# Router logits of a mixture of experts: activations stationary in fp32, or split weights stationary with two tiles' rows streaming

## The chip, the core and the metric

The kernel runs on one core of a Trainium2 chip. The metric is the device time of one launch in microseconds (us). Three launches of the kernel before took 1594.85, 1598.17 and 1599.75 us, and their median, 1598.17 us, is the time before. Engines are named as in the profile: PE is TensorE, PEld its weight loads, DVE VectorE, ACT ScalarE, POOL GpSimd, and SP SyncE, which here only issues DMAs.

## What is computed

One decoder layer on 1024 rows of 2048 columns: a modulated norm, an input projection, spatial gating and stick-breaking attention, an output projection with a residual, and a mixture of 32 experts of which each row takes two. The part around the change is the output projection and the router:

```python
x = x + gate1 * (y @ w_out[l])                                  # y: (1024, 1024), w_out: (1024, 2048)
h = rms_norm(x, norm2_g[l]) * (1.0 + scale2) + shift2
...
g_logits = hf @ w_group + b_group                               # 4 groups
g_idx = argmax(g_logits)
e_logits = (hf @ w_route + b_route).reshape(n, 4, 8)            # 32 experts
top_val, top_idx = top_k(e_logits[g_idx], 2)
...
x = x + gate2 * m                                               # m: the two experts' outputs, weighted
```

All of it is float32. A large product is made in three passes of a split type (float32r): each factor becomes a high part (a copy that is rounded) and a low part (the rest), and high x high, high x low and low x high are summed.

## The kernel before, in words

The output projection is a plan of 32 tiles, `plan = [(cg, t) ...]`: four column groups cg of 512 columns, and in each the eight row tiles t of 128 rows. Below, tile i stands for (cg, t) with i = 8 cg + t. For each tile `mm_out` issues 24 matmuls of 512 columns, three passes for each of eight row chunks of `w_out` (n_ = 0 to 7), and between these eight steps it calls what the dictionary `between` holds. Then `evac_out` and `Piece` take the tile out on VectorE: og = acc x gate1, xi = x + og (the new residual), u = xi x arow (the row for the router and the experts, before its norm). `prev.store` sends xi and u to memory.

The order of all this is written out by hand and recorded under a manual schedule; every engine takes its instructions in that order. In column groups 0 to 2 the piece of the tile before is turned behind step 3 (`turn`: four transposes on PE and a copy uT on ACT) and its logits are made behind step 5 (`logits`: four chunks of 128 columns, the turned rows stationary, 36 columns of router weights streaming, in float32, which PE runs as two passes each). In column group 3 these stand behind steps 2 and 4, and the routing of the tiles before stands among them (`Tail`: `pick1` and `pick2` on VectorE, `exps`, `ranks`, `weights`, `onehots`). All logits are summed in one PSUM bank `lg`, 36 columns for each row tile.

Beside this the same stage also does the following. VectorE makes the experts' output gate (`Gate2.step`, four accumulations of 128x512 at each of the tiles 3 to 18; `Gate2.turn` at tiles 7, 11, 15 and 19, and at tile 19 the last sums go back through PE). `wo_split` prepares the next column group's weights (a high part on ACT, a low part on VectorE): one piece behind tiles 1 and 3 of a group, and two in the middle of tile 7 (`split_late`). `wo_gate` scales the last group's weights on VectorE in column group 2. In column group 0 `ya_turn` brings in the gMLP's rows, with a subtraction on GpSimd for each tile. At tile 8 VectorE makes the router's bias sums cbs, and TensorE uses them ahead of tile 9.

SyncE's queue holds the loads and stores of column groups 0 to 2 and behind them the experts' weights `wx`, 1 MB at a time, in twelve buffers that take the memory of the projection's pools as these come free. GpSimd's queue holds the loads and stores of group 3 and the gathers of the experts' rows. Experts then run one after the other: gather, scale, transposes, three-pass gate and up products, and the down product.

The lines that the following speaks of: `mm_out` L867; og and xi L881 to L884, u L895; the turn L906 and its copy L908; logits L913; the gate's steps L951 and their transposes L936; wo_split's copy L835 and low part L836; gMLP low part L854; cbs L1120 and its product L1124; pick1's first step L990; weights' loads L1240 and L1247; the gather L1220.

Of the kernel before, what the change touches and what calls it, by code (L numbers as in the profile page):

```python
# [17 lines left out]
P = 128  # L18
# [40 lines left out]
def body(ctx, tc, A, out):  # L59
# [580 lines left out]
    with ExitStack() as c3:  # L640
# [4 lines left out]
        class Chain:  # L645
# [78 lines left out]
            def fin0(self):  # L724
                self.y = op.tile([P, 512], F32, name="u3", bufs=3)
                SC.activation(self.y, self.yp, AF.Copy)
                self.sq = op.tile([P, 512], F32, name="og")
                SC.activation(self.sq, self.y, AF.Square)
# [91 lines left out]

    ws_ = c2.enter_context(tc.tile_pool(name="ws", bufs=6, reuse_waits="tile"))
    c5 = ExitStack()
    rt = c5.enter_context(tc.tile_pool(name="rt", bufs=1, side="right", reuse_waits="tile"))
# [66 lines left out]
    class Piece:  # L890
        def __init__(self, cg, t, x, g):
            self.cg, self.t, self.g = cg, t, g
            cs = slice(cg * 512, (cg + 1) * 512)
            self.u = op.tile([P, 512], F32, name="u3", bufs=3)
            V.tensor_tensor(self.u, x, arow[:, cs], op=ALU.mult)  # L895
            self.x = x
# [6 lines left out]
        def turn(self):  # L903
            p = pot.tile([P, 4, P], F32, name="tr2")
            for j in range(4):
                T.transpose(p[:, j, :], self.u[:, j * P:(j + 1) * P], ident)  # L906
            self.uT = self.g.rearrange("p (j q) -> p j q", j=4)
            SC.activation(self.uT, p, AF.Copy)  # L908

        def logits(self):  # L910
            for j in range(4):
                c = self.cg * 4 + j
                T.matmul(lg[:, self.t * 36:(self.t + 1) * 36], self.uT[:, j, :], wgr[:, c, :],  # L913
                         start=(self.t == 0 and c == 0), stop=(c == 15), skip_group_check=True)


    class Gate2:
        def __init__(self):
            self.n, self.t, self.p = 0, [], None
            self.acc = big.tile([P, 8, HALF], F32, name="xk")  # L920
            for i in range(2):
                self.load(i)
# [15 lines left out]
        def step(self):  # L938
# [14 lines left out]
            elif self.n == 16:  # L953
                p = pot.tile([P, 4, P], F32, name="tr2")
                T.transpose(p[0:16, 0, :], g2c, ident)
                r = self.acc[0:16, 1, 0:P]
                SC.activation(r, p[0:16, 0, :], AF.Copy)
                SY.dma_start(mod_d[M_G2:M_G2 + 1, :].rearrange("o (c p) -> (o c) p", p=P), r)
            self.n += 1

    class Tail:
# [24 lines left out]
        def pick1(self):  # L986
            t = self.t
            self.el = rt.tile([P, 36], F32, name="el", bufs=3)
            el = self.el
            V.scalar_tensor_tensor(el, lg[:, t * 36:(t + 1) * 36], self.r, cB, op0=ALU.mult, op1=ALU.add)  # L990
            yield
# [80 lines left out]
    if True:  # L1072
# [19 lines left out]
        wo_load(5)  # L1092
        lg = pol.tile([P, 512], F32, name="lg")

# [11 lines left out]
        for i in range(2):  # L1106
            xin[plan[i]] = x_in(*plan[i])
        tails, prev = {}, None
        g2 = Gate2()
        for i, (cg, t) in enumerate(plan):  # L1110
            if i + 2 < len(plan):
# [26 lines left out]
            x = xin.pop((cg, t))  # L1138
            between = {3: prev.turn, 5: prev.logits} if prev else {}
            if i >= 3 and g2.n <= 16:  # L1140
# [3 lines left out]
            if cg < 3 and t == 7:  # L1144
# [7 lines left out]
                between[4] = split_late(None, cg * 4 + 6)  # L1152
                between[5] = split_late(between[5], cg * 4 + 7)
            if cg == 3:
                between = {2: prev.turn, 4: prev.logits}
                if t >= 2:
                    between[3] = tails[t - 2].exps
# [7 lines left out]
            for n in (4, 5, 6) if i == 0 else ():  # L1165
                fin(n)
            prev = Piece(cg, t, x, evac_out(cg, t, acc, x))
            if cg < 3:
# [358 lines left out]
```

## Time and profile before

| | |
|---|---|
| median of three launches | 1598.17 us (1594.85 to 1599.75) |
| the profiled execution's own time | 1600.44 us |
| its span, first to last instruction | 1598.6 us |
| mean granted clock of TensorE | 0.977 |
| PE busy | 1510.7 us, 95% of the span |
| DVE busy | 1214.8 us, 76% |
| ACT busy | 956.8 us, 60% |
| POOL busy | 299.3 us, 19% |
| logits, L913 | 256 matmuls, 32.2 us busy, 681.7 to 914.8 us |

All times in the rows below are from this one profiled execution, in us from the span's start, and single operations in ns or us as the row says. A granted clock of 1.00 is 2.4 GHz, 0.50 is 1.2 GHz. In a timeline a row is: start, duration, engine, line, operation, output<-inputs, shape, count, and in brackets the idle time of the engine before it with what ended it. The rows of a timeline merge equal neighbours, so the distance between two starts says more of TensorE's pace than a duration, since its matmuls overlap. The output projection lies between 661 and 911 us, the experts between 931 and 1590 us.

### The profile page before, as it was taken

What the parts mean: (1) busy time and instruction counts of PE and PEld (TensorE: products, weight loads), DVE (VectorE), ACT (ScalarE), POOL (GpSimd) and SP (SyncE); (2) the same over time, 40 slices, a digit from 0 to 9 for tenths busy, and PEclk for the clock granted to TensorE, in tenths of its full rate; (3) what the DMA queues carried; (4) which work ended last, traced back from release to release, by engine and by line L of the source; (5) the groups of instructions that cost most, each with busy time, mean ns of one, the idle gap of its engine ahead of it and who ended that gap; (6) DMA issues with size and microseconds to landing.
All of it is one profiled execution on the core that took longest, in us unless ns stands there. A gap on an engine that the chain in (4) does not pass through costs nothing.

```text
span 1598.6 us, 21113 instructions
## 1 busy us (share of the span) xinstructions
PE 1510.7 (95%) x6706; PEld 1137.5 (71%) x6706; DVE 1214.8 (76%) x2214; ACT 956.8 (60%) x2032; POOL 299.3 (19%) x277
## 2 busy tenths in 40 slices
PE   5999998999999899899999879999999999999996
PEld 4788887788888655488878766666666666666663
DVE  5889675867787598758765778888888888887783
ACT  5442588764544598522223477777777777776671
POOL 2000132010011234220001213232211122313021
PEclk9899999999999999999999979999999999999998
DMA  9987478678876000468857559999999999999992
GB/s 378 353 323 239 156 253 300 237 245 295 299 267 228 31 1 1 159 210 297 293 187 290 211 217 329 366 364 377 356 382 355 363 361 355 351 373 346 353 320 37
DMA packets 94408, 433.92 MB, mean 271 GB/s; under 512 B 13088, under 2 KB 13200, under 8 KB 64208
## 3 DMA queue, kind: packets, MB, share of 16 engines
q1 hardware_dynamic: 82000, 377.54, 64.0%
q0 software_dynamic: 12000, 52.85, 11.3%
q10 hardware_dynamic: 288, 2.10, 0.3%
q8 instruction: 55, 0.90, 0.2%
q14 instruction: 65, 0.53, 0.1%
HBM read 400.16 MB, written 43.02 MB: 277 GB/s over the span
## 4 chain that ended last, share of the span: by engine, by line
PE 69%; DMA 10%; ACT 7%; issue 6%; DVE 5%; POOL 2%; SPq 0%; POOLq 0%; ACTq 0%; DVEq 0%; another core or an unknown queue 0%
PE acc L323 22%; PE gu L1291 16%; PE dn L1314 10%; PE acc L867 10%; DMA out<-y,idx 4%; DMA xg<-u_d,idx 3%; PE tp L1265 3%; DMA wm<-in_w_mod 2%; PE lg L913 1%; DVE macc L183 1%; PE tr L906 1%; PE z L657 1%; POOL sl L685 1%; ACT junk L348 1%; ACT wh L1281 1%
## 5 line engine op out<-in xcount | busy, mean ns | idle before, releaser
L1282 DVE TENSOR_TENSOR wl<-wx,wh 128x1024 fp32r<-128x1024 f32 x256 | 309.5, 1219 | 14.6 <-ACT wh L1281 13.5
L1281 ACT ACTIVATE wh<-wx 128x1024 fp32r<-128x1024 f32 x256 | 273.5, 1071 | 37.5 <-PE gu L1291 35.9
L1314 PE MATMUL dn<-wx,actT 128*128 128x512 f32 x512 | 241.5, 595 | 3.1 <-DMA wx<-in_w_down 2.5
L1291 PE MATMUL gu<-wh,xh 128*128 128x512 f32 x512 | 239.4, 468 | 0.0
L183 DVE SCALAR_TENSOR_TENSOR macc<-wm,sc_c,macc 128x512 f32<-128x512 f32 x296 | 222.1, 750 | 11.1 <-DMA wm<-in_w_mod 2.9
L323 PE MATMUL acc<-wh,hh 128*128 128x512 f32 x640 | 209.7, 398 | 3.3 <-ACT hh L279 1.8
L323 PE MATMUL acc<-wl,hh 128*128 128x512 f32 x640 | 206.8, 393 | 2.8 <-DVE wl L308 2.6
L323 PE MATMUL acc<-wh,hl 128*128 128x512 f32 x640 | 206.1, 392 | 0.8 <-DVE hl L280 0.8
L1291 PE MATMUL gu<-wl,xh 128*128 128x512 f32 x512 | 203.1, 397 | 0.2
L1291 PE MATMUL gu<-wh,xl 128*128 128x512 f32 x512 | 202.1, 395 | 0.0
L1224 POOL DMA_INDIRECT out<-y,idx x52 | 94.2, 1812 | 446.6 <-DVE y L1315 440.5
L867 PE MATMUL acc<-wo,yh 128*128 128x512 f32 x512 | 171.3, 416 | 0.0
L1315 DVE TENSOR_TENSOR y<-dn,gate 128x512 f32<-128x512 f32 x128 | 88.5, 691 | 107.8 <-PE dn L1314 107.8
L1270 ACT ACTIVATE xh<-tp,b2c 128x128 fp32r<-128x128 f32 x512 | 146.5, 383 | 21.5 <-PE tp L1265 21.5
L1314 PEld LDWEIGHTS dn<-wx,actT 128*128 128x128 f32 x512 | 96.5, 189 | 79.2 <-issue 63.0
L1272 DVE SCALAR_TENSOR_TENSOR xl<-tp,b2c,xh 128x128 fp32r<-128x128 f32 x512 | 143.3, 343 | 4.3 <-ACT xh L1270 4.3
L323 PEld LDWEIGHTS acc<-wl,hh 128*128 128x128 f32 x640 | 120.9, 190 | 30.0 <-DVE wl L308 4.9
L323 PEld LDWEIGHTS acc<-wh,hl 128*128 128x128 f32 x640 | 121.2, 189 | 27.3 <-DVE hl L280 1.5
L323 PEld LDWEIGHTS acc<-wh,hh 128*128 128x128 f32 x640 | 119.1, 189 | 27.3 <-ACT hh L279 1.9
L308 DVE TENSOR_TENSOR wl<-w,wh 128x1024 fp32r<-128x1024 f32 x80 | 97.5, 1220 | 33.9 <-ACT wh L307 33.8
L307 ACT ACTIVATE wh<-w 128x1024 fp32r<-128x1024 f32 x80 | 82.9, 1053 | 63.7 <-PE acc L323 51.8
L1291 PEld LDWEIGHTS gu<-wl,xh 128*128 128x128 f32 x512 | 97.4, 190 | 30.5 <-issue 14.8
(248 smaller groups left out, 2290.3 us busy)
## 6 DMA issues: line engine op xcount, KB each, us to landing
wx<-in_w_gu SPq DMA_DIRECT2D x128, 1024.0 KB, 23.6
wm<-in_w_mod SPq DMA_DIRECT2D x160, 512.0 KB, 5.5
wx<-in_w_down SPq DMA_DIRECT2D x64, 1024.0 KB, 22.0
w<-in_w_in SPq DMA_DIRECT2D x80, 512.0 KB, 5.4
x<-in_w_mod SPq DMA_DIRECT2D x16, 1024.0 KB, 6.7
wo<-in_w_out SPq DMA_DIRECT2D x16, 512.0 KB, 4.9
xi<-in_x SPq DMA_DIRECT2D x24, 256.0 KB, 6.2
out<-xi SPq DMA_DIRECT2D x24, 256.0 KB, 4.8
```

What stands on the lines that cost most here:

```text
L183: V.scalar_tensor_tensor(self.acc, t[:, j, :], sc, self.acc, op0=ALU.mult, op1=ALU.add)
L308: V.tensor_tensor(wl, w, wh.bitcast(F32), op=ALU.subtract)
L323: T.matmul(accs[t], a, b, start=(first and j == 0 and n == 0), stop=(last and j == 1 and n == 2))
L867: T.matmul(acc, y[a][:, c, ts_], w[b][:, c % 2, :], start=(n_ == 0 and i == 0), stop=(n_ == 7 and i == 2))
L1224: return G.indirect_dma_start(out=out, out_offset=bass.IndirectOffsetOnAxis(ap=idx, axis=0), in_=y, in_offset=None, bounds_check=S - 1, oo ...
L1270: SC.activation(xh[:, j, :], self.p[:, j, :], AF.Identity, bias=b2c[:, b * 4 + j:b * 4 + j + 1])
L1272: V.scalar_tensor_tensor(xl[:, j, :], self.p[:, j, :], b2c[:, b * 4 + j:b * 4 + j + 1], xh[:, j, :].bitcast(F32), op0=ALU.add, op1=ALU.sub ...
L1281: SC.activation(self.wh[q], w, AF.Copy)
L1282: low = lambda: V.tensor_tensor(self.wl[q], w, self.wh[q].bitcast(F32), op=ALU.subtract)
L1291: T.matmul(self.gu, a[c // 4][:, c % 4, :], b[q][:, k, :], start=(c == 0 and i == 0), stop=(c == 15 and i == 2))
L1314: T.matmul(d, self.aT[:, f, :], self.wd[f][:, cs], start=(f == 0), stop=(f == 1))
L1315: V.tensor_tensor(self.y[:, cs], d, gate2[:, cs], op=ALU.mult)
```

## The change

For the first three column groups the logits are made the other way round. The router's weights are split once into a high and a low part, side by side (`whl`: 36 + 36 columns for each of twelve chunks), and are the stationary factor. `turn` now also copies the turned rows in the split type (h, on ACT) and subtracts (l, on GpSimd), into a buffer `pair` with room for two row tiles. Behind step 1 of every odd tile `logits2` streams both tiles' rows, 256 columns: for each of four chunks one matmul of h with all 72 columns and one of l with the 36 high ones. The sums stand turned, 72 partitions by 512 rows, in two banks `lgT`. At tile 25 the last pair is made (`last`), ACT copies both banks to SBUF, and `fold` turns them back by eight float32 matmuls with two stacked identities (`two`), which also adds the high and the low part; column group 3 adds its logits on top as before. At tile 25 these logits stand behind step 6, at tile 24 there are none.

Buffers: the gate's sums move to a new small pool `lp`, and `pair` and `whl` take the memory in which they stood (`g2.parts`); u3 has two buffers in place of three; the attention's last rows y use the ring xi.

```diff
             def fin0(self):
-                self.y = op.tile([P, 512], F32, name="u3", bufs=3)
+                self.y = op.tile([P, 512], F32, name="xi", bufs=4)
...
+    lp = c2.enter_context(tc.tile_pool(name="lp", bufs=1, reuse_waits="tile"))
...
-            self.u = op.tile([P, 512], F32, name="u3", bufs=3)
+            self.u = op.tile([P, 512], F32, name="u3")
...
             self.uT = self.g.rearrange("p (j q) -> p j q", j=4)
+            if self.cg < 3:
+                h, l = (a[:, :, self.t % 2 * P:self.t % 2 * P + P] for a in pair)
+                SC.activation(h, p, AF.Copy)
+                SC.activation(self.uT, p, AF.Copy)
+                G.tensor_tensor(l, self.uT, h.bitcast(F32), op=ALU.subtract)
+                return
             SC.activation(self.uT, p, AF.Copy)
+        def logits2(self):
+            o = lgT[self.t // 4][:, (self.t % 4 - 1) * P:(self.t % 4 + 1) * P]
+            for j in range(4):
+                c = self.cg * 4 + j
+                T.matmul(o[0:72], whl[:, c, :], pair[0][:, j, :], start=(self.t % 4 == 1 and c == 0),
+                         stop=False, skip_group_check=True)
+                T.matmul(o[0:36], whl[:, c, 0:36], pair[1][:, j, :], start=False, stop=(c == 11),
+                         skip_group_check=True)
...
-            self.acc = big.tile([P, 8, HALF], F32, name="xk")
+            self.parts = big.tile([P, 8, HALF], F32R, name="xk")
+            self.acc = lp.tile([P, 1, 512], F32, name="gacc")
...
+        SC.activation(whl[:, :, 0:36], wgr[:, 0:12, :], AF.Copy)
+        G.tensor_tensor(whl[:, :, 36:72], wgr[:, 0:12, :], whl[:, :, 0:36].bitcast(F32), op=ALU.subtract)
+        G.tensor_tensor(two, ident[:, 0:36], ident[:, 36:72], op=ALU.add)
...
-            between = {3: prev.turn, 5: prev.logits} if prev else {}
+            between = {3: prev.turn} if prev else {}
+            if i == 2:
+                lgT[0] = py.tile([P, 512], F32, name="yp")
+            if i >= 3 and i % 2:
+                between[1] = older.logits2
...
                 between[4] = split_late(None, cg * 4 + 6)
-                between[5] = split_late(between[5], cg * 4 + 7)
+                between[5] = split_late(None, cg * 4 + 7)
             if cg == 3:
                 between = {2: prev.turn, 4: prev.logits}
+                if t == 0:
+                    between = {2: prev.turn}
+                if t == 1:
+                    def fold():
+                        lgq.append(pol.tile([P, 512], F32, name="lg"))
+                        for k in range(NT):
+                            T.matmul(lgq[0][:, k * 36:(k + 1) * 36], lgs[0:72, k * P:(k + 1) * P], two[0:72, :],
+                                     start=(k == 0), stop=False, skip_group_check=True)
+
+                    def last():
+                        older.logits2()
+                        for h in range(2):
+                            SC.activation(lgs[0:72, h * HALF:(h + 1) * HALF], lgT[h][0:72, :], AF.Copy)
+                    lgs = gate1[:, 0:S]
+                    between = {0: last, 2: prev.turn, 4: fold, 6: prev.logits}
...
-            prev = Piece(cg, t, x, evac_out(cg, t, acc, x))
+            older, prev = prev, Piece(cg, t, x, evac_out(cg, t, acc, x))
```

The order on three engines, first TensorE at the beginning of tile 9 (the tiles acc; cbs is the bias product ahead of it, tr the turn of tile 8, lg the logits). Before:

```order
L1124 MATMUL acc_6524<-cbs,cst 128x36 x2
L867 MATMUL acc_6528<-wo,yh_4731 128x512 x2
...
L906 MATMUL tr_6541<-cst,u_6512 128x128 x4
L867 MATMUL acc_6528<-wo,yh_4731 128x512 x2
L867 MATMUL acc_6528<-wo,yl_4732 128x512
L867 MATMUL acc_6528<-wo,yh_4731 128x512 x2
L867 MATMUL acc_6528<-wo,yl_4732 128x512
L913 MATMUL lg<-wgr,og 128x36 x4
```

And now, where xk holds whl and the pair of tiles 6 and 7, and the bank lg the turned sums:

```order
L1150 MATMUL acc_6541<-cbs,cst 128x36 x2
...
L868 MATMUL acc_6545<-wo,yh_4731 128x512 x2
L868 MATMUL acc_6545<-wo,yl_4732 128x512
L923 MATMUL lg<-xk 72x256
L925 MATMUL lg<-xk 36x256
L923 MATMUL lg<-xk 72x256
L925 MATMUL lg<-xk 36x256
...
L868 MATMUL acc_6545<-wo,yh_4731 128x512 x2
...
L907 MATMUL tr_6566<-cst,u_6529 128x128 x4
```

Four float32 products behind step 5 are gone (they stood in each tile), and eight products of 256 columns stand behind step 1 of each odd tile, ahead of the turn.

ScalarE from tile 6's evacuation to tile 8's (og<-tr is the copy uT, wo the two late weight splits, og,xss the row sums at an evacuation). Before:

```order
L885 ACTIVATE og,xss_5907<-xi 128x512
L908 ACTIVATE og<-tr_6411 128x512
L835 ACTIVATE wo<-wo 128x1024 x2
L885 ACTIVATE og,xss_5908<-xi 128x512
L908 ACTIVATE og<-tr_6486 128x512
```

And now, with the new copy h written to xk:

```order
L886 ACTIVATE og,xss_5910<-xi 128x512
L911 ACTIVATE xk<-tr_6432 128x4x128
L912 ACTIVATE og<-tr_6432 128x512
L836 ACTIVATE wo<-wo 128x1024 x2
L886 ACTIVATE og,xss_5911<-xi 128x512
```

One copy more stands between the turn and the two weight splits.

SyncE's first loads of expert weights, with the engines whose semaphores each waits for (DMAHW are its own earlier transfers). Before:

```order
L1240 DMA wx<-in_w_gu 128x2048 [waits DMAHW6_49,PE_49]
L1240 DMA wx<-in_w_gu 128x2048 [waits DMAHW7_49]
L1240 DMA wx<-in_w_gu 128x2048 [waits DMAHW0_49]
L1240 DMA wx<-in_w_gu 128x2048 [waits DMAHW1_49]
L1240 DMA wx<-in_w_gu 128x2048 [waits DMAHW2_49,PE_49]
L1240 DMA wx<-in_w_gu 128x2048 [waits DMAHW3_49]
...
L1240 DMA wx<-in_w_gu 128x2048 [waits DMAHW4_49,Activation_49]
L1240 DMA wx<-in_w_gu 128x2048 [waits DMAHW5_49,PE_49]
L1247 DMA wx<-in_w_down 128x2048 [waits DMAHW6_49,PE_49]
```

And now:

```order
L1285 DMA wx<-in_w_gu 128x2048 [waits DMAHW6_49,PE_49,Pool_49]
L1285 DMA wx<-in_w_gu 128x2048 [waits DMAHW7_49]
L1285 DMA wx<-in_w_gu 128x2048 [waits DMAHW0_49]
L1285 DMA wx<-in_w_gu 128x2048 [waits DMAHW1_49]
L1285 DMA wx<-in_w_gu 128x2048 [waits DMAHW2_49]
L1285 DMA wx<-in_w_gu 128x2048 [waits DMAHW3_49,PE_49]
...
L1285 DMA wx<-in_w_gu 128x2048 [waits DMAHW4_49]
L1285 DMA wx<-in_w_gu 128x2048 [waits DMAHW5_49]
L1292 DMA wx<-in_w_down 128x2048 [waits DMAHW6_49]
```

The first load now waits for the last pair product and GpSimd's subtraction before it. The sixth waits for TensorE's matmul of the last tile for which the twelfth waited before; the sixth to the twelfth wait for nothing else.

## Rows read from the trace of the kernel before

**Rows 1.** The page, busy time by engine (share, instructions).

```profile
PE 1510.7 (95%) x6706; PEld 1137.5 (71%) x6706; DVE 1214.8 (76%) x2214; ACT 956.8 (60%) x2032; POOL 299.3 (19%) x277
```

**Rows 2.** Stretches: PE, PEld, DVE, ACT, POOL busy; clock, DMA share, GB/s.

```profile
780.00:810.00 30.00, 30.00 (x162) 25.26 (x161) 25.57 (x35) 8.14 (x15) 0.00 (x0) 1.00 0.86 288
...
1000.00:1060.00 60.00, 60.00 (x247) 41.48 (x246) 49.76 (x87) 45.34 (x91) 15.07 (x10) 1.00 1.01 369
```

**Rows 3.** Timeline of PE around one tile's logits.

```profile
765.97 0.98 PE L913 MATMUL lg<-wgr,og 128*128 128x36 f32 x8
766.77 0.71 PE L867 MATMUL acc<-wo,yh 128*128 128x512 f32 x2
767.32 0.40 PE L867 MATMUL acc<-wo,yl 128*128 128x512 f32 x1
767.55 0.63 PE L867 MATMUL acc<-wo,yh 128*128 128x512 f32 x2
768.02 0.39 PE L867 MATMUL acc<-wo,yl 128*128 128x512 f32 x1
```

**Rows 4.** Timeline of PE in the attention, split type, 256 columns.

```profile
546.79 0.28 PE L710 MATMUL cum<-sh,comp_r 128*128 128x256 f32 x1
546.91 0.28 PE L711 MATMUL cum<-sl,comp_r 128*128 128x256 f32 x1
```

**Rows 5.** Timelines of POOL and DVE, with and without a GpSimd subtraction.

```profile
720.48 1.84 POOL L854 TENSOR_TENSOR yl<-yld,yh 128x512 fp32r<-128x512 f32 x1 [4.98 <-ACT yh L853]
...
719.65 4.01 DVE L951 SCALAR_TENSOR_TENSOR xk<-x,sc_c,xk 128x512 f32<-128x512 f32 x4
...
726.62 3.11 DVE L951 SCALAR_TENSOR_TENSOR xk<-x,sc_c,xk 128x512 f32<-128x512 f32 x4
```

**Rows 6.** Timeline of DVE, column group 0, then group 2.

```profile
712.84 3.99 DVE L951 SCALAR_TENSOR_TENSOR xk<-x,sc_c,xk 128x512 f32<-128x512 f32 x4
716.99 0.69 DVE L881 TENSOR_TENSOR og<-acc,xk 128x512 f32<-128x512 f32 x1 [0.16 <-PE acc L867]
...
803.63 0.69 DVE L881 TENSOR_TENSOR og<-acc,xk 128x512 f32<-128x512 f32 x1 [0.72 <-PE acc L867]
...
810.48 0.69 DVE L881 TENSOR_TENSOR og<-acc,xk 128x512 f32<-128x512 f32 x1 [0.55 <-PE acc L867]
```

**Rows 7.** Timelines of DVE and PE, tiles 7 to 9.

```profile
729.65 2.35 DVE L836 TENSOR_TENSOR wo<-wo 128x1024 fp32r<-128x1024 f32 x2
...
733.37 0.69 DVE L895 TENSOR_TENSOR u<-xi,xk 128x512 f32<-128x512 f32 x1
...
734.45 0.60 PE L906 MATMUL tr<-cst,u 128*128 128x128 f32 x4
...
739.78 0.41 PE L1124 MATMUL acc<-cbs,cst 128*128 128x36 f32 x2 [0.63 <-DVE cbs L1120]
```

**Rows 8.** Timeline of PE, waits behind tiles 19 and in 24.

```profile
820.55 0.27 PE L955 MATMUL tr<-cst,g2c 128*16 128x128 f32 x1 [2.75 <-DVE g2c L942]
...
852.60 0.63 PE L906 MATMUL tr<-cst,u 128*128 128x128 f32 x4 [0.45 <-DVE u L895]
```

**Rows 9.** Timeline of DVE, choice of group and evacuation at tile 25.

```profile
862.50 0.25 DVE L990 SCALAR_TENSOR_TENSOR el<-lg,rs_col,cB 128x36 f32<-128x36 f32 x1 [2.99 <-PE lg L913]
...
865.73 0.69 DVE L895 TENSOR_TENSOR u<-xi,xk 128x512 f32<-128x512 f32 x1
```

**Rows 10.** Timeline of SyncE's queue, the experts' first weights.

```profile
852.89 27.11 SPq L1240 DMA_DIRECT2D wx<-in_w_gu  x8
880.10 0.86 SPq L1247 DMA_DIRECT2D wx<-in_w_down  x2
...
911.12 0.33 SPq L1240 DMA_DIRECT2D wx<-in_w_gu  x1
```

**Rows 11.** The chain that ended last; then DMA issues, 1360 to 1420, us to landing.

```profile
924.89 5.47 DMA xg<-u_d,xss
...
xg<-u_d,idx POOLq DMA_INDIRECT x6, 12.0
```

More of the change, by code (lines that the diff above doesn't have):

```diff
@@ L912, in logits @@
                 c = self.cg * 4 + j
-                T.matmul(lg[:, self.t * 36:(self.t + 1) * 36], self.uT[:, j, :], wgr[:, c, :],
-                         start=(self.t == 0 and c == 0), stop=(c == 15), skip_group_check=True)
+                T.matmul(lgq[0][:, self.t * 36:(self.t + 1) * 36], self.uT[:, j, :], wgr[:, c, :],
+                         start=False, stop=(c == 15), skip_group_check=True)
     class Gate2:
@@ L955, in step @@
                 T.transpose(p[0:16, 0, :], g2c, ident)
-                r = self.acc[0:16, 1, 0:P]
+                r = self.acc[0:16, 0, 0:P]
                 SC.activation(r, p[0:16, 0, :], AF.Copy)
@@ L989, in pick1 @@
             el = self.el
-            V.scalar_tensor_tensor(el, lg[:, t * 36:(t + 1) * 36], self.r, cB, op0=ALU.mult, op1=ALU.add)
+            V.scalar_tensor_tensor(el, lgq[0][:, t * 36:(t + 1) * 36], self.r, cB, op0=ALU.mult, op1=ALU.add)
             yield
@@ L1092, in body @@
         wo_load(5)
-        lg = pol.tile([P, 512], F32, name="lg")
+        lgT = [None, pol.tile([P, 512], F32, name="lg")]
         def lockstep(gens):
@@ L1107, in body @@
             xin[plan[i]] = x_in(*plan[i])
-        tails, prev = {}, None
+        tails, prev, older, lgq = {}, None, None, []
         g2 = Gate2()
+        pair = [g2.parts[:, k:k + 2, :].rearrange("p a (b q) -> p (a b) q", b=2) for k in (0, 2)]
+        whl = g2.parts[:, 4:6, :].rearrange("p a n -> p (a n)")[:, 0:12 * 72].rearrange("p (c e) -> p c e", c=12)
+        two = lp.tile([P, 36], F32, name="two")
+        SC.activation(whl[:, :, 0:36], wgr[:, 0:12, :], AF.Copy)
+        G.tensor_tensor(whl[:, :, 36:72], wgr[:, 0:12, :], whl[:, :, 0:36].bitcast(F32), op=ALU.subtract)
+        G.tensor_tensor(two, ident[:, 0:36], ident[:, 36:72], op=ALU.add)
         for i, (cg, t) in enumerate(plan):
```

## The prediction

> **What bounds the kernel now.** I read the table of stretches first, then the timeline of each engine in the output projection, then the queue of SyncE. In the projection TensorE is busy 30.00 of 30 us, VectorE 25.57, and the DMA engines 0.86 [rows 2]; among the experts TensorE is busy 60.00 of 60 us with the DMA engines at 1.01 [rows 2]. So TensorE sets the end in both, its 1510.7 us [rows 1] have hardly a gap, and what the projection gains or loses goes straight to the end, as long as the experts' first rows arrive as they do now. VectorE is the engine to watch: in column group 0 it idles 0.16 us before a tile's evacuation, in group 2 0.55 us, with tiles 6.85 us apart [rows 6].
>
> **What goes from TensorE.** One tile's logits are 8 passes: from 765.97 to 766.77, 0.80 us, and the pair of matmuls behind them takes 0.55 instead of 0.47 (767.55 to 768.02), so 0.88 us [rows 3]. 24 pieces lose them: 24 x 0.88 = 21.1 us.
>
> **What comes to TensorE.** Twelve pair products of 8 matmuls, 256 columns each, in the split type. The trace has such matmuls in the attention: they start 0.12 us apart [rows 4], with 128 stationary columns, where the new ones have 72 or 36. So 0.96 us and again 0.09 for the change of stream: 1.05 us. Bounds: 0.85 us if the narrower stationary is cheaper, 1.9 us if each took the 0.235 us of half a 512-column pair [rows 3]; I take the row of the same width. 12 x 1.05 = 12.6 us. The turning back is 8 matmuls of two passes each with 36 columns, as the old logits: 16 x 0.10 + 0.08 = 1.7 us (1.2 if they cost less behind each other). Sum on TensorE: -21.1 + 12.6 + 1.7 = **-6.8 us**. Even tiles become 0.88 shorter, odd tiles 0.17 longer.
>
> **What comes to the others.** ScalarE makes one more 512-column copy per piece, some 0.5 us. It has room, but its order matters at three tiles, below. GpSimd gets 24 subtractions of 128x512; the same operation takes 1.84 us in the trace, next to VectorE [rows 5]. The buffer changes (u3 two deep, the attention's rows in xi, the small pool lp) move no wait that I find: the rows that they delay are asked for a tile later, and an x tile lands long before. They cost nothing while that holds, and a few tenths if not.
>
> **The price of the subtractions.** Four accumulation steps of the gate vector take 3.11 us on VectorE when GpSimd is idle (726.62), and 4.01 us when GpSimd's subtraction at 720.48 falls among them [rows 5]; 3.99 us at 712.84 [rows 6]. So one subtraction among such steps costs VectorE 0.90 us. This is the Trainium skill's rule in "SBUF — State Buffer", section "Who interferes with whom": a VectorE instruction with both inputs in SBUF contends with a GpSimd instruction that reads SBUF. The rows above agree. By its opposite, that only VectorE's copies meet GpSimd, these subtractions would cost nothing and the sum would end at the first rival. Nearly each of the new subtractions of tiles 3 to 19 falls among the steps: the transposes stand 2.8 us into a tile (3.85 in an odd one, behind the pair product), two copies and the semaphores later it is 4.7 (5.7), and VectorE's steps and weight low parts run from about 2.2 to 5.3 us and on to 6.5 us where a low part follows.
>
> **Where it reaches the path.** VectorE needs 2.1 us for evacuation (three operations of 0.69 [rows 6, 7]), 3.1 for the steps, up to 1.2 for a low part or a weight scaling, and now 0.9: up to 7.3 us against a mean tile of 6.5 on TensorE. Place by place:
> - Tiles 3 to 6, group 0. VectorE also scales the gMLP rows here and has 0.16 us left [rows 6]. Three subtractions add 2.7 us. By the plain sum tile 8 would start 3.0 us earlier (7 x 0.88 - 3 x 1.05); with VectorE as the pace I expect it 0.5 later. Loss 3.5.
> - Tiles 7 to 9. Tile 7's turn stands 1.05 later behind the pair product and ScalarE has the extra copy 0.5, so its two weight splits come 1.55 later and VectorE's low parts (729.65) 1.25 later; then u, now ready at 734.06, is ready at 735.4, where TensorE wants it at 734.6 (734.45 now) [rows 7]. TensorE already waits 0.63 us at 739.78 for VectorE's sums cbs [rows 7], and one more subtraction falls before them: VectorE is 2.3 later where TensorE would be 0.7 earlier. Loss 3.0 for both.
> - Tile 16, the same splits without cbs: loss 1.2.
> - Tiles 17 to 19: VectorE idles 0.55 us [rows 6], and each tile adds 0.9 where TensorE takes 0.4 less in the mean; the wait of 2.75 us at 820.55 for the gate's last sums [rows 8] hangs on the same engine. Loss 3.0.
> - Tile 24, the same splits: the wait of 0.45 us at 852.60 [rows 8] grows by 1.4.
> - Tile 26: tile 24's logits move behind the turning back, from the fifth place of tile 25 to the seventh. VectorE's choice of the group starts behind the logits, at 862.50, and runs until the evacuation, 2.5 us; that evacuation's u stands at 865.73 [rows 9]. In the changed order it starts 0.5 us before the tile's end. Loss 1.4.
> Sum of the losses 13.5 us, bounds 0 and 16: none if VectorE keeps up everywhere, 16 if every subtraction costs its 0.9. I take 13.5, since the rows with such a collision are of these very instructions. Projection: -6.8 + 13.5 = **+6.7 us**.
>
> **The experts' weights.** Of the first twelve loads eight go out from 852.89, two at 880.10, one behind them, and the twelfth at 911.12, with the projection's last matmul [rows 10]. In the changed program the order of the buffers is another: five loads are free early in column group 3, the sixth waits for the matmul for which the twelfth waits now, and seven queue behind it on SyncE. These are 7.3 MB; at the 369 GB/s of rows 2 they take 20 us from the last matmul. The weights themselves should be in time, as expert 0's four are among the five early ones and expert 1 comes an expert later. But the gather of expert 0's rows is issued 13.8 us after it and stands on the path with 5.47 us; among full queues gathers land after 12.0 us in the median [rows 11]. So the gather costs between 0 and 6.5 us more; I take **+2.5**, since only the last third of the burst meets it. The Trainium skill ("DMA: Bandwidth & Descriptors", section "Queues, rings and completion order") says that each DMA engine goes round-robin between its queues by packets; by that the gather would share and not queue behind all seven, which bears the middle value out. No row here shows the arbitration itself.
>
> **Sum.** +6.7 + 2.5 = +9.2 us on the profiled execution's 1600.44 us, so 1609.6. That execution is 2.3 us above the median of 1598.17, so against the median I say **1607 us**.
>
> **Rivals.**
> 1. GpSimd's subtractions don't hold VectorE up, or fall beside the steps. Then only the late splits (0.8 at tile 8, 1.2 at cbs, 0.8 at tile 16, 1.4 at tile 24) and tile 26 (1.4) remain, 5.6 us: -6.8 + 5.6 + 2.5 = +1.3, that is 1599.5. For it: VectorE has 4.4 us of 30 free in rows 2. Against: rows 5.
> 2. Faster: TensorE keeps its gain. VectorE catches up within a tile, since three evacuation buffers let TensorE run ahead and the turn stands well into a tile; the gather is not held up either. -6.8, so 1591.4. It decides if VectorE's idle time before an evacuation in group 2 stays above 0. For it: TensorE is busy without a gap in rows 2 although VectorE is nearly full there. Against: the turn needs the last u, so TensorE may run ahead by 2.8 us at most.
> 3. The burst is worse than I think: the gather takes the 12.0 us of full queues, +6.5 in place of +2.5, and the projection stands as forecast: 1611. For it: seven loads on SyncE's queue at once. Against: the burst has at most 6 us left when the gather starts.
>
> **Chances.** Forecast 0.45, rival 1 0.28, rival 2 0.14, rival 3 0.13. A measurement here can tell about 0.3%, 4.8 us, from no change. Rival 2 is faster by that; rival 1 lies within; forecast and rival 3 are slower, but the forecast's lower edge, where a third of its losses is missing, falls within: faster 0.14, same 0.32, slower 0.54. Forecast's own range 1602 to 1612. For 8 in 10 I take 1594 to 1613: below lies most of rival 2, above only a gather and all collisions together.
>
> **What would show it.** Pair products 0.12 us apart; VectorE's four steps near 4.0 us in most tiles of groups 0 to 2; its idle time before og gone in tiles 4 to 7 and 17 to 19; TensorE waiting for u at tiles 8, 16, 24 and 26 and longer for cbs; five weight loads before the projection's end, seven behind it; the gather longer than 5.5 us. I am wrong if the steps stay at 3.1 us, if the pair products start 0.2 us apart, or if TensorE waits for the subtractions themselves, which end about 1 us before they are wanted.

## The result, and the profile after

The changed kernel takes 1606.64 us (median of 7 runs, 1603.3 to 1610.91), the kernel before 1596.74 us (7 runs, 1593.23 to 1599.75): a ratio of 1.0068, 95% interval 1.0051 to 1.0084, so 8 to 13 us slower. The profiled execution of the changed kernel took 1606.64 us, its span is 1604.9 us. Line numbers below are those of the changed kernel: L923 and L925 the pair products, L913 GpSimd's subtraction, L970 the gate's steps, L882 and L885 the first operation of an evacuation (og, and xi in group 3), L896 u, L907 the turn, L1192 the fold.

Busy time by engine, after (share of the span, instructions), to be read against [rows 1]:

```profile
PE 1499.7 (93%) x6626; PEld 1124.1 (70%) x6626; DVE 1228.2 (77%) x2214; ACT 969.4 (60%) x2059; POOL 334.5 (21%) x303
```

TensorE is busy 11.0 us less on this page (by the distances of its rows the saving is 8.2 us, below) and the kernel is slower, so the gain turned into waits. The longest waits of TensorE from 660 to 925 us, after (engine, line <- waited for: us in total, times, longest):

```profile
PE tr L907 <- ACT og L886: 6.1, 6, 2.1
PE tr L974 <- DVE g2c L961: 3.4, 1, 3.4
PE tr L907 <- DVE u L896: 3.1, 3, 1.6
...
PE acc L1150 <- DVE cbs L1146: 2.8, 2, 2.2
```

The first line is a trap in reading. The turn doesn't need ScalarE's row sum og; it needs u, which VectorE ends at about the same moment. Where the profile names u, the turn follows its end by 0.06 us (below: u from 872.46 to 873.15, turn at 873.21, while that tile's row sum ends only at 873.24) or by 0.15 us (726.42 and 726.57); where it names og, the turn stands 0.15 us behind the end of u as well (855.96 and 856.11). So the first and the third line are one wait, for VectorE's evacuation. Before the change all waits for u came to 2.0 us in two places.

The pair products, the fold and two late turns in TensorE's timeline, after (start, duration, engine, line, operation, output<-inputs, in brackets the idle time before):

```profile
856.11 0.63 PE L907 MATMUL tr<-cst,u 128*128 128x128 f32 x4 [2.07 <-ACT og L886]
...
860.81 0.28 PE L923 MATMUL lg<-xk 128*72 128x256 f32 x1
860.92 0.28 PE L925 MATMUL lg<-xk 128*36 128x256 f32 x1
...
861.74 0.62 PE L868 MATMUL acc<-wo,yh 128*128 128x512 f32 x2
...
864.97 1.87 PE L1192 MATMUL lg<-two,xk 72*128 72x36 f32 x16
866.68 0.70 PE L868 MATMUL acc<-wo,yh 128*128 128x512 f32 x2
...
869.50 0.40 PE L868 MATMUL acc<-wo,yl 128*128 128x512 f32 x1
...
873.21 0.66 PE L907 MATMUL tr<-cst,u 128*128 128x128 f32 x4 [1.21 <-DVE u L896]
```

Pair products start 0.11 to 0.12 us apart, one of the 96 waits for GpSimd, for 0.2 us, and the next tile product comes 0.93 us after the first of the eight (861.74); the fold takes 1.71 us until 866.68. The row of 869.50 is the last product of tile 25. Tile 24's wait, 0.45 us in [rows 8], is 2.07 us, and tile 26 has a new one of 1.21 us. VectorE at that place, after, to be read against [rows 9]:

```profile
869.23 0.26 DVE L1009 SCALAR_TENSOR_TENSOR el<-lg,rs_col,cB 128x36 f32<-128x36 f32 x1 [7.04 <-PE lg L931]
...
871.74 0.68 DVE L885 TENSOR_TENSOR xi<-xi,acc 128x512 f32<-128x512 f32 x1
872.46 0.69 DVE L896 TENSOR_TENSOR u<-xi,xk 128x512 f32<-128x512 f32 x1
```

VectorE is idle for 7.04 us, then the choice of the group fills the last 2.5 us before the evacuation, which starts 1.8 us after the end of TensorE's last product of the tile (869.50 + 0.40). Now VectorE and GpSimd in group 0, after, against [rows 5, 6]:

```profile
719.44 4.93 DVE L970 SCALAR_TENSOR_TENSOR gacc<-x,sc_c,gacc 128x512 f32<-128x512 f32 x4
724.29 0.68 DVE L882 TENSOR_TENSOR og<-acc,xk 128x512 f32<-128x512 f32 x1
725.73 0.69 DVE L896 TENSOR_TENSOR u<-xi,xk 128x512 f32<-128x512 f32 x1
726.34 4.03 DVE L970 SCALAR_TENSOR_TENSOR gacc<-x,sc_c,gacc 128x512 f32<-128x512 f32 x4
```

```profile
720.27 1.86 POOL L855 TENSOR_TENSOR yl<-yld,yh 128x512 fp32r<-128x512 f32 x1 [3.95 <-ACT yh L854]
722.08 1.74 POOL L913 TENSOR_TENSOR xk<-og,xk 128x512 fp32r<-128x512 f32 x1
728.46 1.37 POOL L913 TENSOR_TENSOR xk<-og,xk 128x512 fp32r<-128x512 f32 x1 [4.63 <-ACT og L912]
```

Two GpSimd subtractions inside four steps make them 4.93 us, one makes them 4.03, none 3.11 [rows 5]: 0.90 to 0.92 us each. Taken one by one, the second and third of the four steps of 719.44 show where it falls:

```profile
720.22 0.75 DVE L970 SCALAR_TENSOR_TENSOR gacc<-x,sc_c,gacc 128x512 f32<-128x512 f32 x1
721.01 1.67 DVE L970 SCALAR_TENSOR_TENSOR gacc<-x,sc_c,gacc 128x512 f32<-128x512 f32 x1
```

The step that is running when a subtraction starts (720.27) keeps its 0.75 us; the next one, which starts while the subtraction runs, takes 1.67. So a subtraction lengthens one step. The bracket before og is gone: VectorE goes from steps to evacuation to steps without a pause.

The chain at the gather, and SyncE's weight loads, after, against [rows 10, 11]:

```profile
931.57 9.53 DMA xg<-u_d,xss
```

```profile
861.97 2.41 SPq L1285 DMA_DIRECT2D wx<-in_w_gu  x5
...
917.76 0.80 SPq L1285 DMA_DIRECT2D wx<-in_w_gu  x2
918.13 0.91 SPq L1285 DMA_DIRECT2D wx<-in_w_gu  x2
919.08 1.20 SPq L1292 DMA_DIRECT2D wx<-in_w_down  x2
920.32 29.13 SPq L1285 DMA_DIRECT2D wx<-in_w_gu  x4
```

Five loads go out early. Seven stand behind the last matmul: three by the rows of 917.76 and 918.13 (they share a load, since they come from neighbouring stretches), two of 919.08, and the first two of the last row. The gather takes 9.53 us in place of 5.47. It starts 6.68 us later than before, by the projection, and ends 10.74 us later.

The end of the span is only 6.3 us later. From the gather's end to the end of the span the changed kernel takes 663.8 us, the kernel before 668.2. The difference is a wait for a down-projection weight, in the profile of before near 1485 us, which the profile after lacks:

```profile
1485.14 1.12 PE L1314 MATMUL dn<-wx,actT 128*128 128x512 f32 x2 [2.50 <-DMA wx<-in_w_down]
```

It is taken up with the last experiment. The medians, 9.9 us apart, agree with projection and gather, 10.7 us.

### The profile page after: what moved, and what is told of

Same layout as the page of the kernel before. It is cut to its first block, busy times and chain, and to the rows that moved or that the text cites. A ratio compares the mean times of both kernels' runs of the same rounds, so it can differ in the third digit from the quotient of the medians.

```text
span 1604.9 us, 21036 instructions
## 1 busy us (share of the span) xinstructions
PE 1499.7 (93%) x6626; PEld 1124.1 (70%) x6626; DVE 1228.2 (77%) x2214; ACT 969.4 (60%) x2059; POOL 334.5 (21%) x303
## 4 chain that ended last, share of the span: by engine, by line
PE 63%; DMA 11%; DVE 9%; ACT 8%; issue 6%; POOL 2%; SPq 0%; POOLq 0%; DVEq 0%; ACTq 0%; another core or an unknown queue 0%
PE acc L323 22%; PE gu L1336 16%; PE dn L1359 10%; PE acc L868 6%; DMA out<-y,idx 4%; DMA xg<-u_d,idx 3%; PE tp L1310 3%; DMA wm<-in_w_mod 2%; DVE gacc L970 2%; DVE macc L183 1%; PE z L657 1%; ACT junk L348 1%; POOL sl L685 1%; DMA u_d<-u 1%; ACT xh L1315 1%
## 5 line engine op out<-in xcount | busy, mean ns | idle before, releaser
L1327 DVE TENSOR_TENSOR wl<-wx,wh 128x1024 fp32r<-128x1024 f32 x256 | 309.7, 1220 | 15.9 <-ACT wh L1326 14.7
L1298 ACT ACTIVATE xg<-xg,rs 128x512 f32<-128x512 f32 x126 | 92.3, 734 | 44.4 <-DMA xg<-u_d,idx 36.1
```

The costliest lines, as they stand in the source:

```text
L1298: SC.activation(xs, xs, AF.Copy, scale=self.rs)
L1327: low = lambda: V.tensor_tensor(self.wl[q], w, self.wh[q].bitcast(F32), op=ALU.subtract)
```

## Experiments

Each was timed against the kernel before in the same session; ratios have their 95% interval, and line numbers in a run's rows are those of its own kernel. The changed kernel was timed in an earlier session, so a difference from it, or between two edited kernels of different sessions, is one between sessions (medians of the kernel before: 1596.14 to 1597.35 us). Where it is below about 5 us, the rows beside it carry more than the medians. "Tile 9 at 750.53" is the start of that tile's evacuation.

**The subtraction alone, taken away.**

```diff
                 SC.activation(self.uT, p, AF.Copy)
-                G.tensor_tensor(l, self.uT, h.bitcast(F32), op=ALU.subtract)
...
+        for k in (2, 3):
+            G.tensor_tensor(g2.parts[:, k, :], gate1[:, 0:HALF], gate1[:, 0:HALF], op=ALU.subtract)
```

> The changed kernel without the 24 GpSimd subtractions (the low part of the turned rows is written once, as zero, so the logits lack it); ScalarE's two copies stay. Theory (each subtraction that falls among VectorE's two-SBUF steps costs VectorE 0.9 us, and VectorE paces the projection): the four-step groups go back to 3.1 us, the projection ends 7 to 9 us earlier than in the changed kernel, 1598 to 1600 us. Rival (the turn that stands behind the pair product and ScalarE's extra copy make the delay, not the subtraction): steps shorten, but the time stays within 2 us of 1606.6.

Measured: 1598.68 us, ratio 1.0019 (1.0006 to 1.0031), 8.0 us less than the changed kernel. The steps, in this kernel:

```profile
716.69 4.02 DVE L969 SCALAR_TENSOR_TENSOR gacc<-x,sc_c,gacc 128x512 f32<-128x512 f32 x4
722.68 3.11 DVE L969 SCALAR_TENSOR_TENSOR gacc<-x,sc_c,gacc 128x512 f32<-128x512 f32 x4
```

The first still has the gMLP rows' own subtraction among it; the other is back at 3.11 us. From tile 0 to tile 7 this kernel takes 53.10 us, the changed one 57.21. TensorE does the same work in both, so the 8.0 us are what the 24 subtractions cost. The gather still takes 9.85 us here. The rival is out.

**The subtraction alone, added to the kernel before.**

```diff
             SC.activation(self.uT, p, AF.Copy)
+            if self.cg < 3:
+                G.tensor_tensor(g2.acc[:, 2, :], self.g, arow[:, 0:512], op=ALU.subtract)
```

> The kernel before with one GpSimd subtraction of 128x512 added in each of the 24 turns of groups 0 to 2, into a tile that nobody reads. Theory: steps of 4.0 us, VectorE late by 0.9 per tile where it has 0.16 us (group 0, tiles 3 to 6) and 0.55 us (tiles 17 to 19) to spare: about 3 + 1 to 2 + 1 = 4 to 6 us slower, 1600.7 to 1602.7 us. Rival (VectorE catches up within a tile, three evacuation buffers): within 1 us of 1596.7.

Measured: 1600.67 us against 1596.67, ratio 1.0039 (1.0024 to 1.0053), the lower edge of what was expected. Its profiled execution, 1595.36 us, is the shortest of its runs; in it too the projection is longer, 240.37 us from tile 0 to tile 31 against 236.04. Two step groups of VectorE and the GpSimd work near them:

```profile
723.31 4.01 DVE L953 SCALAR_TENSOR_TENSOR xk<-x,sc_c,xk 128x512 f32<-128x512 f32 x4
...
740.13 3.11 DVE L953 SCALAR_TENSOR_TENSOR xk<-x,sc_c,xk 128x512 f32<-128x512 f32 x4
```

```profile
725.00 1.76 POOL L910 TENSOR_TENSOR xk<-og,xk 128x512 f32<-128x512 f32 x1 [4.21 <-ACT og L908]
...
742.78 1.59 POOL L910 TENSOR_TENSOR xk<-og,xk 128x512 f32<-128x512 f32 x1 [8.03 <-ACT og L908]
```

The subtraction at 725.00 lies inside the steps and they take 4.01 us; that at 742.78 starts while the last of them is already running, and they take 3.11. A result that nobody reads costs the kernel 4.0 us.

**The low part on VectorE.**

```diff
                 SC.activation(h, p, AF.Copy)
-                SC.activation(self.uT, p, AF.Copy)
-                G.tensor_tensor(l, self.uT, h.bitcast(F32), op=ALU.subtract)
+                V.tensor_tensor(l, p, h.bitcast(F32), op=ALU.subtract)
```

> The changed kernel with the low part taken by VectorE, straight from PSUM (turned rows minus high part), and neither GpSimd's subtraction nor ScalarE's second copy. Theory (what counts is VectorE's time): 24 x 0.69 = 16.6 us more on VectorE in place of the 13.0 us by which VectorE's busy time grew in the changed kernel's projection, so no better: 1606 to 1610 us. Rival (GpSimd's holding of VectorE is worse than its sum, because it also holds the evacuation that TensorE waits for): 1600 to 1603 us.

Measured: 1599.06 us, ratio 1.0017 (1.0004 to 1.0029), 7.6 us less than the changed kernel. The theory's expectation failed. Its 13.0 us don't come out of the rows: from 660 to 920 us VectorE is busy 180.50 us before and 188.41 after, and the changed kernel is 6.7 us further back by then, so such stretches hold unequal work. Over tiles that match better, VectorE's costliest groups from 700 to 822 us (busy time, mean ns), after:

```profile
L970 DVE SCALAR_TENSOR_TENSOR gacc<-x,sc_c,gacc 128x512 f32<-128x512 f32 x60 | 58.6, 976 | 1.7
...
L837 DVE TENSOR_TENSOR wo<-wo 128x1024 fp32r<-128x1024 f32 x8 | 12.1, 1529 | 0.9 <-ACT wo L836 0.9
```

and with the low part on VectorE:

```profile
L969 DVE SCALAR_TENSOR_TENSOR gacc<-x,sc_c,gacc 128x512 f32<-128x512 f32 x60 | 47.8, 796 | 1.7
...
L912 DVE TENSOR_TENSOR xk<-tr,xk 128x512 fp32r<-128x512 f32 x17 | 11.6, 683 | 2.6 <-ACT xk L911 2.6
L837 DVE TENSOR_TENSOR wo<-wo 128x1024 fp32r<-128x1024 f32 x9 | 10.8, 1220 | 1.8 <-ACT wo L836 1.8
```

The subtractions lengthened steps by 10.8 us and eight weight low parts by 2.5 (8 x 0.31): 13.3 us for about 17 of them, 0.78 each. Done by VectorE itself, one stands 0.60 us from start to start. That is 3 us for these 17; ScalarE's copy, below, is worth another 2 or so. Some 2 us of the 7.6 stay without a row; tile 9, which loses to a lower clock after the change (last section) and doesn't here, may hold them, but that isn't shown.

**The loads early.**

```diff
-    wpools = [wpa] * 4 + [wpc] * 2 + [wpr] + [wpb] * 4 + [wpe]
+    wpools = [wpa] * 4 + [wpr] + [wpb] * 4 + [wpc] * 2 + [wpe]
```

> The changed kernel with the experts' weight buffers taken in another order, so that ten of the first twelve loads are free before the projection's last matmul and two behind it (five and seven in the changed kernel). Theory (the burst of seven loads holds the gather of expert 0's rows): gather back from 9.5 to 5.5-6.5 us, 3 to 4 us faster, 1602.6 to 1603.6 us. Rival (the gather takes 9.5 us for its own reasons, or the loads behind it decide): gather near 9.5 us and 1606.6 us.

Ten of the first twelve loads go out between 859.18 and 886.1 us here, and two from 914.98. Measured: 1603.06 us, ratio 1.005 (1.0035 to 1.0066), 3.6 us less than the changed kernel. The gather:

```profile
928.79 5.44 DMA xg<-u_d,xss
```

**The burst, given to the kernel before.**

```diff
-    wpools = [wpa] * 4 + [wpc] * 2 + [wpr] + [wpb] * 4 + [wpe]
+    wpools = [wpa] * 4 + [wpc, wpe, wpc, wpr] + [wpb] * 4
```

> The kernel before with the experts' weight buffers taken in such an order that the sixth of the first twelve loads waits for the projection's last matmul and six queue behind it, as in the changed kernel; nothing else differs. Theory (the burst of seven loads holds the gather): gather from 5.5 to about 9.5 us, 3.5 to 4.5 us slower than before, 1600.2 to 1601.2 us. Rival (the late gather of the changed kernel has another cause): gather near 5.5 us, within 1 us of 1596.7.

Measured: 1599.47 us against 1596.14, ratio 1.0027 (1.0014 to 1.004): 3.3 us, just under the range given. The gather:

```profile
926.40 9.56 DMA xg<-u_d,xss
```

In both directions the row changes by the same 4.1 us: the late gather comes from the order of the buffers, not from the router.

**Splits and fold ahead.**

```diff
-                between[4] = split_late(None, cg * 4 + 6)
-                between[5] = split_late(None, cg * 4 + 7)
+                between[2] = split_late(None, cg * 4 + 6)
+                between[4] = split_late(None, cg * 4 + 7)
...
-                    between = {0: last, 2: prev.turn, 4: fold, 6: prev.logits}
+                    between = {0: last, 2: prev.turn, 3: fold, 4: prev.logits}
```

> The changed kernel with two moves in program order: in tiles 7, 15 and 23 the first of the two weight splits goes ahead of the turn (step 2) and the second to step 4; in tile 25 the fold goes from step 4 to 3 and tile 24's logits from 6 to 4. Theory (late splits and late logits make TensorE wait at tiles 8, 16, 24 and 26: 0.89, 0.93, 2.07 and 1.21 us in the changed kernel's trace): the wait at 26 goes, that at 24 falls to 0.5, those at 8 and 16 halve; 3 to 4 us faster, 1602.6 to 1603.6 us. Rival (VectorE's steps with the subtractions set the pace there, not ScalarE's order): only tile 26's 1.2 us returns, 1605.4 us.

Measured: 1603.17 us, ratio 1.0055 (1.0036 to 1.0075), 3.5 us less between the medians; this interval overlaps that of the changed kernel, so the size rests on the rows. TensorE's turns at tiles 8, 16 and 24, in this kernel:

```profile
730.28 0.63 PE L907 MATMUL tr<-cst,u 128*128 128x128 f32 x4 [0.89 <-ACT og L886]
...
790.18 0.63 PE L907 MATMUL tr<-cst,u 128*128 128x128 f32 x4 [0.70 <-ACT og L886]
...
850.31 0.63 PE L907 MATMUL tr<-cst,u 128*128 128x128 f32 x4 [1.16 <-ACT og L886]
```

Tile 26's wait is gone, tile 24's fell by 0.91 us, tile 16's by 0.23, tile 8's not at all: together 2.35 us, and from tile 0 to tile 30 the projection is 2.36 us shorter (232.25 against 234.61). By these rows the gain is less than the theory's 3 to 4 us, and places 8 and 16 answer as the rival says, which fits VectorE's own queue being the pace there.

**Without subtraction and without ScalarE's second copy.**

```diff
                 SC.activation(h, p, AF.Copy)
-                SC.activation(self.uT, p, AF.Copy)
-                G.tensor_tensor(l, self.uT, h.bitcast(F32), op=ALU.subtract)
...
+        for k in (2, 3):
+            G.tensor_tensor(g2.parts[:, k, :], gate1[:, 0:HALF], gate1[:, 0:HALF], op=ALU.subtract)
```

> The changed kernel without the 24 GpSimd subtractions and without ScalarE's second copy as well (the low part is written once, as zero, so the logits lack it). Theory (the loss is VectorE's, ScalarE's copy matters only ahead of three pairs of splits at 0.5 us each): 0 to 1.5 us faster than without the subtractions alone, 1597.2 to 1598.7 us. Rival (the extra copy delays more than that, which would be why the low part on VectorE gained more than its 24 x 0.69 us allowed): 1593 to 1596 us.

Measured: 1596.15 us, ratio 0.9999 (0.9987 to 1.001), 2.5 us less than without the subtraction alone (1.0019, 1.0006 to 1.0031). That lies between the two expectations. The two intervals overlap, so it isn't shown that the copy costs more than the 1.5 us allowed. The profiles point that way: without tile 9, which runs at a lower clock in this profile and not in the other, the projection is 2.3 us shorter (59.56 us against 60.80 from tile 0 to tile 8, 162.33 against 163.36 from tile 9 to tile 31). Which of the tiles the copy delays wasn't taken apart.

**All four edits together.** Low part on VectorE, loads early, splits and fold ahead.

> The changed kernel with all four edits: low part on VectorE from PSUM, the weight buffers in the order that lets ten of twelve loads go early, the first split ahead of the turn, and fold and logits earlier in tile 25. Theory (the terms are separate and add): 1599.1 - 3.6 for the gather - 1.2 for tile 26 - 1 to 2 for tiles 16 and 24 = 1592 to 1593 us, 4 us less than before. Rival (VectorE, with the low parts in its queue, sets the pace and hides the order; or the experts then wait for weights): 1595 to 1597 us, no gain over before.

Measured: 1594.38 us against 1596.14, ratio 0.9993 (0.9982 to 1.0004): not to be told from the kernel before, and between the two expectations. What TensorE still waits for, from 660 to 925 us:

```profile
PE tr L907 <- DVE u L896: 3.6, 4, 1.6
PE tr L973 <- DVE g2c L960: 3.6, 1, 3.6
...
PE acc L1149 <- DVE cbs L1145: 1.7, 2, 1.1
```

The kernel before has 2.0, 2.75 [rows 8] and 0.63 us [rows 7] in these places. The next two runs take the last two lines.

**The waits for cbs and g2c moved, in the mended kernel.**

```diff
+        def finish(self):
+            p = pot.tile([P, 4, P], F32, name="tr2")
+            T.transpose(p[0:16, 0, :], g2c, ident)
...
-            elif self.n == 16:
-                p = pot.tile([P, 4, P], F32, name="tr2")
-                T.transpose(p[0:16, 0, :], g2c, ident)
...
-            if (cg, t) == (1, 0):
+            if (cg, t) == (2, 5):
...
-            if (cg, t) == (1, 1):
+            if (cg, t) == (2, 7):
...
+            if i == 20:
+                between[6] = g2.finish
```

> The mended changed kernel (low part on VectorE, loads early, first split ahead, fold earlier) with two pieces of other work moved: the sums cbs from tile 8 to tile 21 (their matmuls from tile 9 to 23), where VectorE idles, and the gate's last turn from the end of tile 19 into tile 20. Theory (what is left of TensorE's gain sits in these two waits, 1.7 us for cbs and 3.6 us for g2c): both waits go, 4 to 5 us less than the mended kernel, 1589.5 to 1590.5 us. Rival (VectorE's pace in tiles 3 to 19 gives it back one wait later): 1593 to 1595 us.

Measured: 1584.13 us against 1597.35, ratio 0.9927 (0.991 to 0.9944): 13 us faster than the kernel before, the best of all, and more than the theory allowed: 10.3 us less than the mended kernel where 4 to 5 were expected. From tile 7 to 8 it is 6.22 us in place of 8.29 (737.81 - 731.59, 737.71 - 729.42), from tile 19 to 20 5.90 in place of 10.66 (817.36 - 811.46, 822.52 - 811.86): 6.8 us, more than the two waits' 5.3 us. The other 3.5 us stay without a row.

**The same moves in the kernel before.** The same moves as in the last diff.

> The kernel before with the same two moves (cbs to tile 21, the gate's last turn into tile 20). Theory: only its own waits go, 0.6 us for cbs and 2.75 us for g2c: 3 us faster, 1593 us; so the split router's own worth against it is what is left between this and the mended kernel with the same moves, 2.5 to 3.5 us. Rival: VectorE, freed of the sums in tile 8, gives more: 1590 to 1591 us, and the split router is worth nothing.

Measured: 1592.92 us against 1597.35, ratio 0.9967 (0.9955 to 0.998), 4.4 us faster where 3 were expected. So of the 13 us 4.4 have nothing to do with the router; the split router, mended, is worth 8.8 us between the medians of the same session, where 2.5 to 3.5 were expected; that is about the 8.2 us that TensorE saves. Why the wait of 2.75 us was worth 4.46 in tile 20 (11.86 us from 817.47 to 829.33 before, 7.40 here) shows in the granted clock. Stretches of 4 us (PE, PEld, DVE, ACT, POOL busy; granted clock, DMA share, GB/s), the kernel before:

```profile
816.00:820.00 4.00, 1.80 (x10) 1.25 (x8) 3.24 (x5) 0.72 (x2) 0.00 (x0) 1.00 0.11 44
820.00:824.00 4.00, 3.45 (x10) 2.76 (x11) 1.60 (x3) 1.21 (x2) 0.00 (x0) 0.62 0.30 111
```

and with the moves:

```profile
816.00:820.00 4.00, 4.00 (x23) 3.32 (x21) 3.67 (x6) 2.00 (x4) 0.00 (x0) 1.00 0.34 131
820.00:824.00 4.00, 4.00 (x24) 3.32 (x23) 0.98 (x2) 0.54 (x2) 0.00 (x0) 1.00 0.62 189
```

TensorE was idle for more than half of one stretch, and in the next the granted clock was 0.62 in the mean, between its two levels of 1.00 and 0.50, and it started 10 matmuls instead of 24.

**The changed kernel once more.** Nothing edited, one run with a profile.

> The changed kernel once more, for a second profile. The first shows no wait for a down-projection weight near 1485 us, where the kernel before waited 2.5 us. Theory (that wait varies from run to run and has nothing to do with the change): it is back, 1 to 2.7 us long, and from the gather's end to the end of the span it takes 665 to 668 us instead of 663.8. Rival (the later start of the experts gives the weights time): again no wait, 664 us.

```profile
1493.80 1.13 PE L1359 MATMUL dn<-wx,actT 128*128 128x512 f32 x2 [1.89 <-DMA wx<-in_w_down]
```

1608.9 us, the wait is back, and from the gather's end (940.63) to the end of the span (1607.1) it takes 666.5 us. In the thirteen profiles here this stretch lies between 663.0 and 668.3 us; the kernel before with the added subtraction has 663.2. So the 663.8 us of the first profile were one run's luck and no gain of the change.

## Why the prediction was right, and where its sizes were off

1607 us was forecast and 1606.64 measured. The steps, by the starts of the evacuations (differences of after less before, with the plain sum of TensorE taken out):

| tiles | loss forecast, us | loss measured, us |
|---|---|---|
| 0 to 7 | 3.5 | 3.7 |
| 8, 9 | 3.0 | 3.5 |
| 10 to 14 | 0 | 0.8 |
| 15 (late splits, seen at 16) | 1.2 | 1.3 |
| 16 to 20 | 3.0 | 2.4 |
| 21 to 24 (late splits) | 1.4 | 1.6 |
| 25 (fold, choice late) | 1.4 | 1.5 |
| sum | 13.5 | 14.7 |

Tile 0 itself starts 0.31 us later after the change; that is in no line of the table.

How a line comes about: tile 9 starts its evacuation at 747.25 before and 750.53 after, tile 7 at 731.92 and 732.57, so 2.63 us are lost; the plain sum gives tile 8 -0.88 and tile 9 -0.88 + 0.93, -0.83 in all, so the loss is 3.46. Part of it is a lower clock behind the longer wait for cbs (last section).

- **TensorE's sum** was forecast at -6.8 us. The logits that go were priced from rows and stay so (-21.1); a pair product takes 0.93 us, not 1.05, since no extra 0.09 follows it: 11.2 us for twelve; the fold takes 1.71 as forecast. So -8.2. Rows of the same operation were the right price, with 128 stationary columns as with 72 and 36.
- **The subtractions' price** of 0.90 us was right, and that VectorE hands it on was shown by taking them away (-8.0 us) and by adding them elsewhere (+4.0). By the Trainium skill, "SBUF — State Buffer", section "Who interferes with whom", a VectorE instruction with two SBUF inputs contends with a GpSimd instruction that reads SBUF, and one with at most one SBUF input, outside VectorE's 2-port modes, doesn't; the trace agrees on both: 4.03 us for steps with a subtraction among them, 3.11 without; and a VectorE instruction of the attention with one input in PSUM (z) takes 0.68 us whether a subtraction of GpSimd runs as it starts (602.50) or not (601.90):

```profile
602.50 0.68 DVE L691 SCALAR_TENSOR_TENSOR ls<-z,e 128x512 f32<-128x512 f32 x1
```

```profile
602.15 1.29 POOL L685 TENSOR_TENSOR sl<-sp,sh 128x512 fp32r<-128x512 f32 x1 [0.45 <-DVE sh L684]
```

- **The places** were right, with tile 8's u wait 0.89 us (0.8 in the text's first rival), tile 24's growth 1.62 (1.4) and tile 26's 1.21 (1.4). VectorE's idle time before og is gone in tiles 4 to 8, as said, and in tiles 10 to 12 and 14 to 19 (tiles 4, 7, 8 and 15 had none before). Too small, by the rows, was what ScalarE's second copy costs: 0.5 us at each pair of splits in the text, some 2 us in all in the experiment above.
- **The gather** was forecast at +2.5 us and took 4.06 us more in the profile (3.6 and 3.3 us in the medians of the two experiments on it). The wrong part was that at most 6 us of the burst are left when the gather starts: the last of the seven loads is issued at 920.85 and lands 21.6 us later, so 10.9 us were left at 931.57, and six of the seven had landed when the gather ended. The bounds, 0 to 6.5, held. Nothing here shows how the queues were served.
- **The rest.** +6.67 in the projection and +4.06 at the gather are 10.7 us. The mechanism was right, but that the number came out to the microsecond is luck: TensorE's saving was 1.4 us larger than forecast and the losses 1.2 us larger, and 1.4 us too high a base (a median of three runs, 1598.17, where seven gave 1596.74) made up for most of a gather 1.6 us too small.

Of the rivals, the first (no loss by the subtractions, 1599.5 us) is near what the run without them measured, 1598.68. The second, that TensorE keeps its gain, became true only after six edits. The third, a gather of 12.0 us, is beyond every profile with the burst: 9.53 to 10.00 us.

## What to carry to other kernels

Before work goes from a full engine to an idle one, look at what the idle engine shares with the next-fullest: here TensorE gave up 8.2 us, and the work put on GpSimd, idle for 80% of the span, cost VectorE more than that, by lengthening VectorE's own steps and not through any wait the profile names for GpSimd. The way to see it is the duration of the neighbour's unchanged operations, not its busy share. And when a buffer's place or order changes, follow the next stage's loads: a rotation of twelve buffers was worth 3.6 us here, with 4.1 us in the gather's row.

## What the runs showed of the hardware

A wait of TensorE can cost more than its length. The 2.75 us at 820.55 cost 4.46, by the clock of 0.62 behind it. After the change the two waits for cbs did the same, in this profile:

```profile
740.00:744.00 4.00, 2.91 (x10) 2.23 (x11) 3.90 (x7) 0.72 (x2) 0.00 (x0) 0.78 0.89 260
744.00:748.00 4.00, 4.00 (x21) 3.40 (x20) 2.51 (x5) 0.26 (x1) 0.00 (x0) 0.80 0.70 238
```

The pair products at 744.05 and 744.27 are 0.21 us apart there, at the lower level. It isn't the same in each run: from tile 8 to 9 the changed kernel took 9.17 and 9.18 us in two profiles, the one with the loads early 7.66 us after the same waits of 2.8 us, at a clock of 1.00.

The contention lengthens both sides: a subtraction of 1.28 us at its shortest takes up to 1.86 us among VectorE's steps, and one step per subtraction takes 1.67 us instead of 0.75. One SBUF input alone doesn't exempt an instruction: the attention's copy into the split type (L684) takes 0.43 us at 551.64 with GpSimd idle, and 1.09 at 552.70 with a subtraction running from 552.24 to 553.51.
